# Two plain f pairs instead of one at the start of each FFN, the first token half first

## The chip, the cores and the metric

The kernel runs on one core of a Trainium2 chip. The metric is the device time of one execution in microseconds (us). The engines are called as the profile calls them: PE (matrix multiply; PEld is its weight load), DVE (vector), ACT (scalar), POOL (GpSimd), SP (the queue that issues all DMAs here).

## The reference, cut to what matters

One transformer block on 1024 tokens of 1024 features in float32: an FFN, a token mixer (two attentions, untouched by this change), a second FFN, a last norm. The change is in the first stage of both FFNs.

```python
def rmsnorm(x, g):
    y = xf * lax.rsqrt(jnp.mean(xf * xf, axis=-1, keepdims=True) + EPS)
    return y * g
def swiglu(h, w1, w3, w2):                 # w1, w3: 1024 x 2816, w2: 2816 x 1024
    return (jax.nn.silu(h @ w1) * (h @ w3)) @ w2
...
    x = x + 0.5 * swiglu(rmsnorm(x, ffn1_norm[l]), ffn1_w1[l], ffn1_w3[l], ffn1_w2[l])
    x = x + token_mix(rmsnorm(x, mix_norm[l]), ...)
    x = x + 0.5 * swiglu(rmsnorm(x, ffn2_norm[l]), ffn2_w1[l], ffn2_w3[l], ffn2_w2[l])
```

## The kernel before

Activations lie with features on the 128 partitions: eight feature tiles k of 128 x 512 for each of two token halves tb (K.x[tb][k]). A float32 product is done as three matmuls: each operand is split into a rounded part hi (ACT copies it, L86) and the rest lo (DVE subtracts, L82), and mm3 (L48) adds hi·hi, hi·lo and lo·hi into one PSUM bank. So "a product over all k" is 24 matmuls of 128 x 512.

**ffn_up (L250) computes silu(h w1) · (h w3)** for 22 tiles f of 128 hidden columns, in 11 pairs of f.

- *The first pair is plain* (L266 to L286): for tb = 0, then tb = 1, for both f, banks u[0] (w1) and u[1] (w3) get 24 matmuls each: 96 matmuls in a half, 192 in the pair. Its weights come as four tiles ws[n] of 512 KB (load_fresh, L193): a DMA into one of two staging buffers (wst), a split into whi and wlo. The first half (tb = 0) does not wait for the norm: it multiplies x·gain, and its results are scaled by R[0] = 1/rms afterwards (L278, L280). The first FFN has these weights loaded ahead (`first`), between the loads of x.
- *The second half needs the normed input.* scale_h (L199) makes x·gain·R for the second half on DVE (L209) and splits it (ACT L86, DVE lo L82); then the same for the first half, with ACT (L206) and POOL (L207) doing the scaling.
- *The other ten pairs are done with seven products instead of eight* (L301 to L343, Strassen-Winograd on 2 x 2 blocks: token halves by feature halves). That needs the sums of input blocks made by right_sums (L226: DVE L239 and L243, POOL L241 and L245, 16 splits into tiles `tf`), in place in the x tiles, and sums of weight blocks (L327 to L330; s1, a21, a11, s4), on DVE in the first such pair, on POOL later. A product is 24 matmuls (L298), so such a pair takes 168 matmuls. Banks X, Y, Z hold two banks each.
- *What sets the order.* The program is written in the order above, but the framework's scheduler puts the instructions of each engine into a fixed order by its own timeline estimate, and adds the waits. Each engine and each DMA queue then runs its list strictly in order. Buffers are reused: a tile waits until the last reader of what lay there has finished. The plain part's results go through banks X (f = 0) and Y (f = 1), in both halves. The raw weight tiles of the seven-product pairs (L291, L292: a21, a22, s1, s4) lie where the x tiles were, so their loads wait for the last reads of x.

ffn_down (L356) multiplies by w2 and is not touched; the mixer neither.

The lines that put the first pair into order:

```python
        for tb in range(NTB):
            for f in range(2):
                u = [bank("XY"[f], m) for m in range(2)]
                ...
            if tb == 0:
                scale_h(K, 0, gi, scale_h(K, 1, gi))
        T = right_sums(K, tp)
```

Of the kernel before, what the change touches and what calls it, by code (L numbers as in the profile page):

```python
# [7 lines left out]
F32 = mybir.dt.float32  # L8
F32R = mybir.dt.float32r
# [6 lines left out]
P = 128  # L16
T = 1024
TB = 512
NTB = 2
HB = 256  # L20
D = 1024
KD = 8
NF = 22
# [17 lines left out]
def open_pool(K, ctx, name, bufs, psum=False, side=None):  # L41
    kw = {"space": PSUM} if psum else {}
    if side:
        kw["side"] = side
    return ctx.enter_context(K.tc.tile_pool(name=name, bufs=bufs, reuse_waits="tile", **kw))
# [39 lines left out]
def split(nc, hi, lo, src):  # L85
    nc.scalar.activation(out=hi, in_=src, func=AF.Copy)  # L86
    return lo_of(nc, lo, src, hi)
# [105 lines left out]
def load_fresh(K, n, src):  # L193
    st = K.wst.tile([P, KD, P], F32, tag="wst", name="wst")
    K.nc.sync.dma_start(out=st, in_=src)
    return split_fresh(K, n, st)
# [29 lines left out]
def right_sums(K, tp):  # L226
    nc = K.nc
    h = KD // 2
    T = [[], [], [], []]

# [6 lines left out]
    for k in range(h):  # L237
# [8 lines left out]
        put(3, k, b21)  # L246
    return T


def ffn_up(K, w13, tp, ctx0, gi, first):  # L250
    nc = K.nc
    h = KD // 2
    ctx = ExitStack()
    ps = open_pool(K, ctx, "up_ps", 1, True, side="right")
    bank = lambda n, m: ps.tile([P, TB], F32, tag=f"{n}{m}", name=n)
    K.nw = 0

    def form(src):
        hi, lo = split_fresh(K, K.nw, src)
        K.nw += 1  # L260
        return hi, lo

    def store(f, tb, t):
        nc.sync.dma_start(out=K.s_a[tb][f], in_=t)

    with ExitStack() as c1:  # L266
        sb = open_pool(K, c1, "up_s", 3, side="right")
        ws = first if first else [load_fresh(K, n, w13[n // 2, n % 2]) for n in range(4)]
        K.nw = 4
        for tb in range(NTB):  # L270
            for f in range(2):
                u = [bank("XY"[f], m) for m in range(2)]
                for m in range(2):
                    for k in range(KD):
                        mm3(nc, u[m], ws[2 * f + k // h], m * h + k % h, K.h[tb][k], k == 0, k == KD - 1)
                t = sb.tile([P, TB], F32, tag="s", name="s")
                if tb == 0:
                    nc.vector.tensor_tensor(out=t, in0=u[0], in1=K.R[0], op=ALU.mult)  # L278
                    order_after(K, nc.scalar.activation(out=t, in_=t, func=AF.Silu), K.rdone)
                    nc.gpsimd.tensor_tensor(out=t, in0=t, in1=K.R[0], op=ALU.mult)  # L280
                else:
                    nc.scalar.activation(out=t, in_=u[0], func=AF.Silu)
                nc.vector.tensor_tensor(out=t, in0=u[1], in1=t, op=ALU.mult)
                store(f, tb, t)
            if tb == 0:
                scale_h(K, 0, gi, scale_h(K, 1, gi))  # L286
        T = right_sums(K, tp)
    ctx0.close()
    with ctx:
        rw = open_pool(K, ctx, "up_raw", 1)  # L290
        po = open_pool(K, ctx, "up_post", 1)  # L291
        raw = lambda n: rw.tile([P, KD, P], F32, tag=n, name=n)  # L292
        B11, B21, B22 = K.h[0][0:h], K.h[0][h:], K.h[1][h:]

        def prod(o, w, m, x, start):
            for k in range(h):
                for i, (a, b) in enumerate(((0, 0), (0, 1), (1, 0))):
                    nc.tensor.matmul(o, lhsT=w[a][:, m * h + k], rhs=x[k][b], start=start and k == 0 and i == 0,  # L298
                                     stop=k == h - 1 and i == 2, skip_group_check=True)

        for fp in range(1, NF // 2):  # L301
            f0, f1 = 2 * fp, 2 * fp + 1
            a11 = K.wst.tile([P, KD, P], F32, tag="wst", name="a11")
            a12 = K.wst.tile([P, KD, P], F32, tag="wst", name="a12")
            a21, a22, s1, s4 = raw("a21"), raw("a22"), raw("s1"), raw("s4")
            for t, f, j in ((a11, f0, 0), (a21, f1, 0), (a22, f1, 1), (a12, f0, 1)):
                nc.sync.dma_start(out=t, in_=w13[f, j])
            u = {}
            for n in ("s1", "u2", "u3", "c21", "c11"):
                for m in range(2):  # L310
                    if n != "c11" or m == 0:
                        u[n, m] = po.tile([P, TB], F32, tag=f"{n}{m}", name=n)
            X, Y, Z = [[bank(n, m) for m in range(2)] for n in "XYZ"]

            w = form(a11)
            for m in range(2):
                prod(X[m], w, m, B11, True)
                nc.scalar.activation(out=u["s1", m], in_=X[m], func=AF.Copy)
            w = form(a12)
            for m in range(2):  # L320
                prod(X[m], w, m, B21, False)
            c = u["c11", 0]
            nc.scalar.activation(out=c, in_=X[0], func=AF.Silu)
            nc.vector.tensor_tensor(out=c, in0=X[1], in1=c, op=ALU.mult)
            store(f0, 0, c)
            se = nc.vector if fp == 1 else nc.gpsimd
            se.tensor_tensor(out=s1, in0=a21, in1=a22, op=ALU.add)  # L327
            se.tensor_tensor(out=a21, in0=a11, in1=a21, op=ALU.subtract)
            se.tensor_tensor(out=a11, in0=s1, in1=a11, op=ALU.subtract)
            se.tensor_tensor(out=s4, in0=a12, in1=a11, op=ALU.subtract)  # L330
            for src, x, n in ((a11, T[1], "u2"), (a21, T[2], "u3"), (a22, T[3], "c21")):
                w = form(src)
                for m in range(2):
                    prod(Y[m], w, m, x, n == "u2")
                    nc.vector.tensor_tensor(out=u[n, m], in0=Y[m], in1=u["s1", m], op=ALU.add)
                if n == "c21":
                    finish_a(K, u[n, 0], u[n, 1], f1, 0, store)
            for src, x, n, f in ((s1, T[0], "u3", f1), (s4, B22, "u2", f0)):
                w = form(src)
                for m in range(2):  # L340
                    prod(Z[m], w, m, x, n == "u3")
                    nc.vector.tensor_tensor(out=u[n, m], in0=Z[m], in1=u[n, m], op=ALU.add)  # L342
                finish_a(K, u[n, 0], u[n, 1], f, 1, store)  # L343
# [77 lines left out]
def ffn(K, w13, w2, ctx0, gi, first, xsrc, after, tail=None):  # L421
    with ExitStack() as ctx:
        if not first:
            K.wpools = [K.whl, open_pool(K, ctx, "whl2", B_W, side="right")]
        with ExitStack() as c1:
            ffn_up(K, w13, open_pool(K, c1, "tf", 1, side="right"), ctx0, gi, first)
        ffn_down(K, w2, xsrc, after, tail)


# [1002 lines left out]
```

## Time and profile before

| | us |
|---|---|
| median of 3 runs | 3072.87 (3072.54 to 3073.18) |
| the profiled execution's own time | 3074.79 |
| its span, first to last instruction | 3072.7 |
| mean granted PE clock over the span | 0.982 |
| PE busy | 2925.8 (95%) |
| DVE / ACT / POOL busy | 1838.1 / 1267.6 / 842.3 |

The profiled execution took 1.92 us more than the median, and 2.09 us of it lie around its span. In a timeline row the first number is the start, the second how long the merged piece lasts; "[7.27 <-ACT hi L86]" says that the engine stood idle for 7.27 us before it and what ended that. Matmul pieces show 0.39 us for one, but they are pipelined: what counts is the distance from start to start.

### The profile page before, as it was taken

The page shows a single profiled execution, that of the slowest core. Times are in us where ns is not written, and L with a number is a line of the kernel's source. Part 1 is how long each engine was busy: PE and PEld are TensorE (multiplying, and loading weights), DVE is VectorE, ACT ScalarE, POOL GpSimd, SP SyncE. Part 2 cuts the span into 40 slices and gives each one's busy share as a digit, 9 for nine tenths or more (in the row PEclk, how much of TensorE's full clock was granted, in tenths as well). Part 3 has the DMA queues.
Part 4 walks back from the last instruction along what each step waited for, and adds up shares of the span by engine and source line. Part 5 has one row for each costly group of instructions (what it writes and reads, how often), then busy time and mean ns, then how long its engine had stood idle before and what let it go on. Part 6 is the DMA issues. An engine that isn't in the chain of part 4 may idle for free.

```text
span 3072.7 us, 39792 instructions
## 1 busy us (share of the span) xinstructions
PE 2925.8 (95%) x14490; PEld 2442.3 (79%) x14490; DVE 1838.1 (60%) x3057; ACT 1267.6 (41%) x2231; POOL 842.3 (27%) x687
## 2 busy tenths in 40 slices
PE   6999999999999999889899999999999899999998
PEld 5788887887888778777788888888777688887887
DVE  7655554445678467667677777766434855555354
ACT  6222223332323245345566666666434322223342
POOL 5333330000035222322233333222332433331000
PEclk9999999999999999999999999999999999999999
DMA  2222226444546645444432234222832122225442
GB/s 103 93 83 83 82 69 235 159 144 140 158 158 224 214 142 181 162 168 155 140 111 83 83 123 149 83 76 89 303 124 91 56 83 83 82 83 199 154 167 66
DMA packets 168643, 397.95 MB, mean 130 GB/s; under 512 B 16000, under 2 KB 34688, under 8 KB 168448
## 3 DMA queue, kind: packets, MB, share of 16 engines
q1 hardware_dynamic: 168448, 395.42, 38.0%
q8 instruction: 114, 1.87, 0.3%
q14 instruction: 81, 0.66, 0.1%
HBM read 274.77 MB, written 120.59 MB: 129 GB/s over the span
## 4 chain that ended last, share of the span: by engine, by line
PE 78%; DVE 8%; DMA 6%; ACT 3%; issue 3%; POOL 2%; SPq 1%; DVEq 0%; ACTq 0%; POOLq 0%
PE Y L298 11%; PE X L298 7%; PE Z L298 7%; PE gm L49 6%; PE gm L51 6%; PE gm L50 6%; PE S L682 6%; PE acc L49 5%; PE acc L51 5%; PE acc L50 5%; PE tr L732 3%; PE o L886 2%; PE o L885 2%; DMA sg<-smx 1%; DMA wst<-in_win_dram 1%
## 5 line engine op out<-in xcount | busy, mean ns | idle before, releaser
L82 DVE TENSOR_TENSOR wlo<-wst,whi 128x1024 fp32r<-128x1024 f32 x183 | 238.1, 1303 | 233.6 <-ACT whi L86 223.3
L49 PE MATMUL gm<-hi,whi 128*128 128x512 f32 x880 | 352.5, 401 | 4.6 <-ACT whi L86 2.1
L51 PE MATMUL gm<-hi,wlo 128*128 128x512 f32 x880 | 348.9, 397 | 0.0
L50 PE MATMUL gm<-lo,whi 128*128 128x512 f32 x880 | 348.6, 396 | 0.0
L682 PE MATMUL S<-kt,qt 128*128 128x320 f32 (+5 forms) x1152 | 274.5, 352 | 44.2 <-ACT Pt L691 16.5
L298 PE MATMUL Y<-tf,whi 128*128 128x512 f32 x960 | 300.2, 394 | 1.0 <-ACT whi L86 1.0
L86 ACT ACTIVATE whi<-wst 128x1024 fp32r<-128x1024 f32 x147 | 155.1, 1058 | 333.0 <-PE acc L50 187.3
L86 ACT ACTIVATE th<-tr 128x512 fp32r<-128x512 f32 (+2 forms) x384 | 204.0, 543 | 200.9 <-PE tr L732 196.5
L82 DVE TENSOR_TENSOR tl<-tr,th 128x512 fp32r<-128x512 f32 (+2 forms) x384 | 236.6, 620 | 82.6 <-ACT th L86 78.9
L49 PE MATMUL acc<-ah,whi 128*128 128x512 f32 (+1 forms) x728 | 280.4, 385 | 4.5 <-DVE u L342 4.5
L51 PE MATMUL acc<-ah,wlo 128*128 128x512 f32 (+1 forms) x728 | 280.3, 385 | 0.0
L50 PE MATMUL acc<-al,whi 128*128 128x512 f32 (+1 forms) x728 | 279.7, 384 | 0.0
L689 DVE CUSTOM_DVE_ANT_0 S<-S,slab 128x896 f32<-128x896 f32 (+7 forms) x320 | 224.9, 709 | 69.3 <-PE S L682 64.0
L682 PEld LDWEIGHTS S<-kt,qt 128*128 128x128 f32 x1152 | 183.5, 190 | 67.8 <-ACT Pt L691 17.7
L839 POOL TENSOR_SCALAR Ps<-Ps,l 128x384 f32<-128x384 f32 (+7 forms) x128 | 100.7, 787 | 422.3 <-DVE l L837 209.9
L298 PEld LDWEIGHTS Y<-tf,whi 128*128 128x128 f32 x960 | 180.7, 188 | 43.0 <-ACT whi L86 1.4
L86 ACT ACTIVATE whi<-a 128x1024 fp32r<-128x1024 f32 x100 | 104.0, 1058 | 233.4 <-PE Y L298 157.7
L49 PEld LDWEIGHTS gm<-hi,whi 128*128 128x128 f32 x880 | 168.6, 192 | 37.5 <-ACT whi L86 2.3
L51 PEld LDWEIGHTS gm<-hi,wlo 128*128 128x128 f32 x880 | 168.2, 191 | 36.0 <-DVE wlo L82 0.3
L50 PEld LDWEIGHTS gm<-lo,whi 128*128 128x128 f32 x880 | 168.3, 191 | 31.5 <-issue 0.5
L82 DVE TENSOR_TENSOR wlo<-a,whi 128x1024 fp32r<-128x1024 f32 x100 | 173.9, 1753 | 26.3 <-ACT whi L86 26.3
L298 PE MATMUL Y<-tf,wlo 128*128 128x512 f32 x480 | 188.6, 394 | 0.0
(302 smaller groups left out, 6683.4 us busy)
## 6 DMA issues: line engine op xcount, KB each, us to landing
wst<-in_win_dram SPq DMA_DIRECT2D x55, 512.0 KB
wst<-in_f1w_dram SPq DMA_DIRECT2D x48, 512.0 KB
wst<-in_f2w_dram SPq DMA_DIRECT2D x48, 512.0 KB
ar<-sa SPq DMA_DIRECT2D x88, 256.0 KB
a<-in_f1w_dram SPq DMA_DIRECT2D x40, 512.0 KB
a<-in_f2w_dram SPq DMA_DIRECT2D x40, 512.0 KB
qt<-sq SPq DMA_DIRECT2D x128, 128.0 KB
qt<-sqn SPq DMA_DIRECT2D x64, 256.0 KB
```

The lines of the kernel that those rows point to most:

```text
L49: first = nc.tensor.matmul(out, lhsT=w[0][:, wk], rhs=x[0], start=start, stop=False, skip_group_check=skip)
L50: nc.tensor.matmul(out, lhsT=w[0][:, wk], rhs=x[1], start=False, stop=False, skip_group_check=skip)
L51: nc.tensor.matmul(out, lhsT=w[1][:, wk], rhs=x[0], start=False, stop=stop, skip_group_check=skip)
L82: return nc.vector.tensor_tensor(out=lo, in0=src, in1=hi.bitcast(F32), op=ALU.subtract)
L86: nc.scalar.activation(out=hi, in_=src, func=AF.Copy)
L298: nc.tensor.matmul(o, lhsT=w[a][:, m * h + k], rhs=x[k][b], start=start and k == 0 and i == 0, stop=k == h - 1 and i == 2, skip_group_chec ...
L682: K.last = nc.tensor.matmul(S[:, o:o + n], lhsT=q, rhs=k[:, k0 + c:k0 + c + n], start=i == 0, stop=i == 1)
L689: nc.vector.tensor_tensor_reduce(out=sv, in0=sv, in1=mv, scale=-0.125, scalar=BIG, op0=ALU.add, op1=ALU.min, accum_out=nm)
L732: nc.tensor.transpose(tr[:, b * P:(b + 1) * P], src, K.ident)
L839: nc.gpsimd.tensor_scalar(out=p[:, 0:n], in0=p[:, 0:n], scalar1=l[:, c:c + 1], scalar2=1.0, op0=ALU.mult, op1=ALU.mult)
L885: nc.tensor.matmul(dst, lhsT=v, rhs=hi[:, b * P:(b + n) * P], start=False, stop=False, skip_group_check=True)
L886: nc.tensor.matmul(dst, lhsT=v, rhs=lo[:, b * P:(b + n) * P], start=False, stop=last, skip_group_check=True)
```

## The change

Two pairs are done plainly instead of one (NPLAIN = 2), eight weight tiles instead of four, and both pairs are done on the first token half before the second half is touched: the order of (tb, pair) is (0,0), (0,1), (1,1), (1,0). The weights of the second pair get a pool of their own (up_w, four pairs of tiles), which is closed before the pool `tf` of the block sums is opened: the sums lie where these weights were. The results go round the three bank sets X, Y, Z. The second half is scaled after (0,0), the first half (in place of its own unscaled split) after (0,1). Nine pairs are left for the seven-product form.

```diff
+def load_plain(K, pools, n, src):
+    st = K.wst.tile([P, KD, P], F32, tag="wst", name="wst")
+    K.nc.sync.dma_start(out=st, in_=src)
+    pool = pools[n % 2] if n < 4 else pools[2]
+    hi = pool.tile([P, KD, P], F32R, tag="whi", name="whi")
+    lo = pool.tile([P, KD, P], F32R, tag="wlo", name="wlo")
+    split(K.nc, hi, lo, st)
+    return hi, lo
+
+NPLAIN = 2
...
-        sb = open_pool(K, c1, "up_s", 3, side="right")
-        ws = first if first else [load_fresh(K, n, w13[n // 2, n % 2]) for n in range(4)]
-        K.nw = 4
-        for tb in range(NTB):
+        plain = K.wpools[:]
+        plain.append(open_pool(K, c1, "up_w", 4, side="right"))
+        sb = open_pool(K, c1, "up_s", 3)
+        ws = [first if first else [load_plain(K, plain, n, w13[n // 2, n % 2]) for n in range(4)]]
+        ws.append([load_plain(K, plain, n, w13[n // 2, n % 2]) for n in range(4, 8)])
+        nu = 0
+        for tb, p in ((0, 0), (0, 1), (1, 1), (1, 0)):
             for f in range(2):
-                u = [bank("XY"[f], m) for m in range(2)]
+                nu += 1
+                u = [bank("XYZ"[nu % 3], m) for m in range(2)]
                 for m in range(2):
                     for k in range(KD):
-                        mm3(nc, u[m], ws[2 * f + k // h], m * h + k % h, K.h[tb][k], k == 0, k == KD - 1)
+                        mm3(nc, u[m], ws[p][2 * f + k // h], m * h + k % h, K.h[tb][k], k == 0, k == KD - 1)
...
-                store(f, tb, t)
-            if tb == 0:
-                scale_h(K, 0, gi, scale_h(K, 1, gi))
-        T = right_sums(K, tp)
+                store(2 * p + f, tb, t)
+            if (tb, p) == (0, 0):
+                gates = scale_h(K, 1, gi)
+            if (tb, p) == (0, 1):
+                scale_h(K, 0, gi, gates)
+    K.nw = 4
+    T = right_sums(K, open_pool(K, ctxt, "tf", 1, side="right"))
...
-        for fp in range(1, NF // 2):
+        for fp in range(NPLAIN, NF // 2):
...
-            se = nc.vector if fp == 1 else nc.gpsimd
+            se = nc.vector if fp == NPLAIN else nc.gpsimd
```

In the changed file the lines stand lower: L278 is L295, L283 is L300, L298 is L318, L307 is L327, L327 is L347; L49 to L245 are the same.

**The order of PE, first FFN, where the first token half ends.** hi_276, lo_277 and hi_349, lo_350 are the first and the last feature tile of the first half's input, whi_271 to wlo_337 the first pair's weights, whi_420 and wlo_421 the first tile of the second pair's. Before:

```order
L50 MATMUL Y_475<-lo_350,whi_336 128x512
L51 MATMUL Y_475<-hi_349,wlo_337 128x512
L49 MATMUL X_618<-hi_531,whi_271 128x512 [waits Activation_49]
L49 MATMUL X_619<-hi_531,whi_271 128x512 [waits DVE_49]
L49 MATMUL Y_672<-hi_531,whi_314 128x512
L49 MATMUL Y_673<-hi_531,whi_314 128x512 [waits DVE_49]
L50 MATMUL X_618<-lo_532,whi_271 128x512 [waits DVE_49]
```

The same place now, and then the end of the second pair's first half:

```order
L50 MATMUL Z_499<-lo_350,whi_336 128x512
L51 MATMUL Z_499<-hi_349,wlo_337 128x512
L49 MATMUL X_594<-hi_276,whi_420 128x512 [waits Activation_49]
L50 MATMUL X_594<-lo_277,whi_420 128x512
L51 MATMUL X_594<-hi_276,wlo_421 128x512
...
L51 MATMUL Y_651<-hi_349,wlo_439 128x512
L49 MATMUL Z_754<-hi_555,whi_420 128x512 [waits Activation_49]
L50 MATMUL Z_754<-lo_556,whi_420 128x512 [waits DVE_49]
```

Before, the second half's input (hi_531, lo_532) was asked for right behind the first half. Now 96 matmuls on the first half's input stand between, and the second half's first tile (hi_555, lo_556) is asked for behind them.

**The order of DVE, first FFN, up to the scaling of the second half.** R_360 and R_402 are 1/rms of the halves; nm, nacc their steps. Before:

```order
L162 TENSOR_SCALAR nm_358<-tot_356 128x512 [waits PE_49]
L120 TENSOR_TENSOR nacc_280<-nacc_280,nm_358 128x512 [waits DVE_49,Activation_49]
L121 TENSOR_SCALAR nacc_280<-nacc_280 128x512 [waits DVE_49]
L122 TENSOR_TENSOR R_360<-R_360,nacc_280 128x512 [waits DVE_49]
L162 TENSOR_SCALAR nm_400<-tot_398 128x512 [waits PE_49]
L278 TENSOR_TENSOR s_468<-X_418,R_360 128x512 [waits DVE_49]
```

And now:

```order
L82 TENSOR_TENSOR wlo_421<-wst_418,whi_420 128x1024 [waits DMAHW5_49,Activation_49]
L151 TENSOR_TENSOR nacc_368<-nacc_368,nsq_395 128x512 [waits DVE_49,Activation_49]
L162 TENSOR_SCALAR nm_358<-tot_356 128x512 [waits PE_49]
L82 TENSOR_TENSOR wlo_427<-wst_424,whi_426 128x1024 [waits DMAHW6_49,Activation_49]
L120 TENSOR_TENSOR nacc_280<-nacc_280,nm_358 128x512 [waits DVE_49,Activation_49]
L121 TENSOR_SCALAR nacc_280<-nacc_280 128x512 [waits DVE_49]
L82 TENSOR_TENSOR wlo_433<-wst_430,whi_432 128x1024 [waits DMAHW7_49,Activation_49]
L122 TENSOR_TENSOR R_360<-R_360,nacc_280 128x512 [waits DVE_49]
L162 TENSOR_SCALAR nm_400<-tot_398 128x512 [waits PE_49]
L82 TENSOR_TENSOR wlo_439<-wst_436,whi_438 128x1024 [waits DMAHW0_49,Activation_49]
L295 TENSOR_TENSOR s_492<-Y_442,R_360 128x512 [waits DVE_49]
```

The four splits of the second pair's weights now stand inside the chain that makes R, each waiting for its load.

**The order of DVE, first FFN, the block sums.** tf tiles are the splits of the block sums, s_858 is the result of (1,1) with f = 1, s_912 that of (1,0) with f = 0, a11 the first seven-product weight. Now:

```order
L243 TENSOR_TENSOR x1_7_267<-x1_7_267,x0_3_264 128x512 [waits Pool_49]
L300 TENSOR_TENSOR s_804<-Z_755,s_804 128x512 [waits DMAHW4_49,PE_49,Activation_49]
L300 TENSOR_TENSOR s_858<-X_809,s_858 128x512 [waits DMAHW5_49,PE_49,Activation_49]
L82 TENSOR_TENSOR tf_977<-x0_0_252,tf_976 128x512 [waits Activation_49]
...
L82 TENSOR_TENSOR tf_1047<-x1_7_267,tf_1046 128x512 [waits Activation_49]
L82 TENSOR_TENSOR wlo_1090<-a11_1064,whi_1089 128x1024 [waits DMAHW1_49,PE_49,Activation_49]
L300 TENSOR_TENSOR s_912<-Y_863,s_912 128x512 [waits DMAHW6_49,PE_49]
```

Before, these splits stood mixed with the sums themselves, from the first sum on. Now twelve of them follow in one row behind the last result of (1,1).

In the mixer, between the two FFNs, no engine's order changes.

## Rows read from the trace of the kernel before

**Rows 1.** The page: busy time by engine, and the shares of the chain that ended last.

```profile
PE 2925.8 (95%) x14490; PEld 2442.3 (79%) x14490; DVE 1838.1 (60%) x3057; ACT 1267.6 (41%) x2231; POOL 842.3 (27%) x687
...
PE 78%; DVE 8%; DMA 6%; ACT 3%; issue 3%; POOL 2%; SPq 1%; DVEq 0%; ACTq 0%; POOLq 0%
```

**Rows 2.** The timeline of PE, first FFN: the rows at which it stops and goes on (start, length, what, idle before it).

```profile
32.45 0.39 PE L51 MATMUL Y<-hi,wlo 128*128 128x512 f32 x1
40.10 1.22 PE L49 MATMUL X<-hi,whi 128*128 128x512 f32 x2 [7.27 <-ACT hi L86]
...
47.72 0.79 PE L49 MATMUL Y<-hi,whi 128*128 128x512 f32 x1 [5.97 <-DVE s L283]
48.80 0.79 PE L50 MATMUL X<-lo,whi 128*128 128x512 f32 x1 [0.29 <-DVE lo L82]
...
72.05 0.50 PE L298 MATMUL X<-hi,whi 128*128 128x512 f32 x1 [0.25 <-ACT whi L86]
...
80.15 0.79 PE L298 MATMUL X<-hi,wlo 128*128 128x512 f32 x1 [7.37 <-DVE wlo L82]
...
81.17 0.63 PE L298 MATMUL X<-lo,whi 128*128 128x512 f32 x1
81.60 0.63 PE L298 MATMUL X<-hi,wlo 128*128 128x512 f32 x1
...
94.58 1.20 PE L298 MATMUL Z<-tf,whi 128*128 128x512 f32 x4 [0.91 <-ACT whi L86]
96.74 1.20 PE L298 MATMUL Y<-tf,whi 128*128 128x512 f32 x4 [0.96 <-ACT whi L86]
99.06 0.54 PE L298 MATMUL Z<-tf,wlo 128*128 128x512 f32 x1 [1.12 <-DVE wlo L82]
...
475.35 0.40 PE L298 MATMUL Z<-hi,wlo 128*128 128x512 f32 x1
```

**Rows 3.** The chain that ended last, first FFN, in order of time (start, length, what): from the second half's norm to the first seven-product matmuls.

```profile
38.26 8.81 DVE x L209 x8
...
47.66 10.87 DVE lo L82 x10
...
59.21 7.70 POOL x L241
...
78.96 1.15 DVE wlo L82
```

**Rows 4.** The instructions of L298 alone in the steady stretch of the first FFN (window, its length, PE busy (count), PEld busy (count), granted clock, DMA share, GB/s).

```profile
126.67:476.00 349.33, 349.07 (x1513) 283.43 (x1511) 1.00 0.25 82
```

**Rows 5.** All engines in a stretch of the first FFN in which PE waits (columns: us, PE, PEld, DVE, ACT, POOL busy with counts, granted clock, DMA share, GB/s).

```profile
40.00:50.00 10.00, 3.64 (x7) 2.12 (x8) 10.00 (x10) 9.67 (x19) 8.38 (x6) 0.50 0.07 26
```

**Rows 6.** The timeline of PE, second FFN.

```profile
2357.76 0.47 PE L49 MATMUL X<-hi,whi 128*128 128x512 f32 x1
...
2380.81 0.61 PE L49 MATMUL X<-hi,whi 128*128 128x512 f32 x2
2385.54 0.50 PE L50 MATMUL X<-lo,whi 128*128 128x512 f32 x1 [4.12 <-DVE lo L82]
...
2409.33 0.39 PE L298 MATMUL X<-hi,whi 128*128 128x512 f32 x1
...
2411.83 0.39 PE L298 MATMUL X<-hi,wlo 128*128 128x512 f32 x1
2416.19 0.50 PE L298 MATMUL X<-hi,whi 128*128 128x512 f32 x1 [3.98 <-DVE s L283]
...
2424.51 0.50 PE L298 MATMUL X<-hi,whi 128*128 128x512 f32 x1 [0.66 <-ACT s L318]
...
2432.08 2.08 PE L298 MATMUL Z<-tf,whi 128*128 128x512 f32 x4 [4.50 <-ACT whi L86]
...
2811.11 0.40 PE L298 MATMUL Z<-hi,wlo 128*128 128x512 f32 x1
```

**Rows 7.** Loads of 512 KB: the SP queue's issues in the first FFN (two of a, the first when the first buffer is free), and one piece of the chain in the second FFN (issue to landing of two such loads together).

```profile
18.50 6.42 SPq L307 DMA_DIRECT2D a<-in_f1w_dram  x2
...
2422.98 4.41 DMA a<-in_f2w_dram
```

**Rows 8.** The timeline of DVE: splits of weights (wlo), of the second half's input (lo) and of block sums (tf), and its idle time in the norm's chain of the first FFN.

```profile
23.35 1.22 DVE L82 TENSOR_TENSOR wlo<-wst,whi 128x1024 fp32r<-128x1024 f32 x1
25.75 1.49 DVE L151 TENSOR_TENSOR nacc<-nacc,nsq 128x512 f32<-128x512 f32 x2 [1.18 <-POOL nacc L151]
...
29.86 0.69 DVE L120 TENSOR_TENSOR nacc<-nacc,nm 128x512 f32<-128x512 f32 x1 [2.03 <-ACT nacc L119]
...
47.59 10.94 DVE L82 TENSOR_TENSOR lo<-x,hi 128x512 fp32r<-128x512 f32 x10
...
59.05 0.68 DVE L82 TENSOR_TENSOR lo<-x,hi 128x512 fp32r<-128x512 f32 x1
59.65 0.68 DVE L239 TENSOR_TENSOR x<-x,x 128x512 f32<-128x512 f32 x1
...
68.63 3.49 DVE L82 TENSOR_TENSOR tf<-x,tf 128x512 fp32r<-128x512 f32 x2
```

**Rows 9.** The timeline of POOL, first FFN: scalings of the first half beside the splits of rows 8.

```profile
48.42 6.55 POOL L207 TENSOR_TENSOR x<-x,R 128x512 f32<-128x512 f32 x4 [0.22 <-ACT x L206]
```

**Rows 10.** Groups of DVE instructions from 36 to 90 us (count | busy us, mean ns | idle before).

```profile
L82 DVE TENSOR_TENSOR tf<-x,tf 128x512 fp32r<-128x512 f32 x16 | 14.6, 954 | 0.0
```

More of the change, by code (lines that the diff above doesn't have):

```diff
@@ L247, in right_sums, with ffn_up @@
     return T
-def ffn_up(K, w13, tp, ctx0, gi, first):
+def load_plain(K, pools, n, src):
[7 more added lines that the diff above has]
+NPLAIN = 2
+def ffn_up(K, w13, ctxt, ctx0, gi, first):
     nc = K.nc
@@ L425, in ffn @@
         with ExitStack() as c1:
-            ffn_up(K, w13, open_pool(K, c1, "tf", 1, side="right"), ctx0, gi, first)
+            ffn_up(K, w13, c1, ctx0, gi, first)
         ffn_down(K, w2, xsrc, after, tail)
```

## The prediction

> **What bounds the kernel.** PE is busy for 95% of the span and holds 78% of the chain that ended last [rows 1]. So a change pays where PE stands idle or runs slowly, and costs where PE gets more matmuls. I went from the page to PE's timeline at the beginning of each FFN, for its holes and what ended them; to the chain of waits there, for what fills the holes; to the timelines of DVE, POOL and SP, for what the new order asks of them; and to the order of the changed program, for what is late next.
>
> In the first FFN PE ends the plain pair's first half at 32.7 us and then stands still for 7.27 us, does four matmuls, stands still for 5.97 us, and again for 7.37 us behind the second matmul of the seven-product part [rows 2]. The chain shows why: norm, 8.81 us of scaling on DVE, 10.87 us of splits, then sums, then the split of a weight that is queued behind them [rows 3]. From 40 to 50 us DVE is busy all the time and PE for 3.64 us [rows 5]. After a hole PE also runs at half its clock for some microseconds: the granted clock is 0.50, the 1.2 GHz level, in the stretch with the holes [rows 5], and after the last one matmuls start 0.43 us apart [rows 2]. The second FFN has the same holes, shorter: 4.12, 3.98, 0.66 and 4.50 us [rows 6]. Elsewhere the seven-product part is dense: 1513 matmuls from 126.67 to 475.58 us, **0.2306 us each** [rows 2, 4]. I use that pitch throughout.
>
> **What the change adds.** A plain pair has 192 matmuls, a seven-product pair 168. So each FFN gets 24 more: 24 x 0.2306 = 5.5 us, all on PE, 11.1 us in both. Further splits and results of the plain pair on DVE, ACT and POOL take the place of weight sums and results of the pair they replace; they count only where they delay the chain (below). DMA traffic is the same eight weight tiles, moved earlier.
>
> **What it removes.** 96 matmuls that need nothing new are put where PE had to wait. I compare the moment at which the seven-product part ends.
>
> First FFN, before: 32.7 us to the end of the first half, end at 475.6 us [rows 2]. In between lie 96 + 1680 matmuls, 409.5 us at the steady pitch; so 33.4 us are lost, of which the holes listed in rows 2 make 24.1 and slow matmuls behind them the rest. After, without any hole: 32.7 + 288 x 0.2306 = 99.1 us to the end of the plain pairs, + 1512 x 0.2306 = 348.7, end at 447.8 us. **Gain 27.8 us**, the 24 added matmuls included.
>
> Second FFN, before: first half ends at 2380.8, the end is at 2811.3 us [rows 6]; less 409.5 us that leaves 21.0 us lost. After: 2380.8 + 66.4 + 348.7 = 2795.9. **Gain 15.4 us.** Together 43.2 us, if PE never waits.
>
> **Does it never wait?** I put the new order's lists beside the durations, place by place.
>
> *The second pair's weights.* Four more tiles of 512 KB go through the two staging buffers, ahead of the loads of a. The first can be issued at 18.5 us, when a buffer is free; two loads took 4.41 us together [rows 7], so I take 2.2 to 4.4 us for one. The first is split by about 26 to 28 us, the last by 36 to 38; PE asks for them at 32.7, 35.5, 43.8 and 46.5. No wait.
>
> *The norm's chain in the first FFN.* These four splits (1.13 us each on DVE, about what [rows 8] shows start to start) now stand inside it, and ACT and DVE wait in order for the loads. Part falls into DVE's idle time of 1.18 and 2.03 us [rows 8]. Walking down both lists, the scaling begins at 40.3 us (short loads) to 42.5 us (long ones) in place of 38.3 [rows 3]. Add 8.8 us of scaling and two results: the eight splits lo of the second half begin at 50.3 to 52.5 us. With ten of them in 10.94 us [rows 8] the last is ready at 59 to 61.2. PE comes to the second half at 32.7 + 22.1 = 54.8 and needs the last of the eight tiles at 59.7. So between 0 and 1.5 us of waiting; I take 1.5, since these loads meet those of x.
>
> *The same in the second FFN.* R is made later there, since DVE waits for a product of POOL ahead of it: scaling begins at 2380.4 to 2381.6, the last split is done by 2402.3; PE comes at 2403.0 and needs that one at 2407.7. No wait.
>
> *The first half's new splits* may be written only when (0,1) has been read, and have the 22.1 us of (1,1) for some 14 DVE instructions of 0.6 to 1.1 us: no wait.
>
> *The block sums' splits* lie where the second pair's weights were, so they begin after (1,1), at 77 us in the first FFN, with the 22.1 us of (1,0) before them. Twelve splits at 0.95 us [rows 10], two results and two weight splits take some 15 us; PE needs the first weight at 99.1 and the first sum 11 us later. Then the loads of a21 and a22 wait for the last four splits: issued by 97, landed 4.41 us later [rows 7], three sums and a split: ready at about 106, needed at 110. No wait. The bank set of (1,1), X, is free long before the seven-product part begins on it: that wait of 3.98 us [rows 6] ends.
>
> For small waits in the first seven-product pairs I add 0.5 us. **Sum:** 43.2 - 1.5 - 0.5 = 41.2 us. The profiled execution took 3074.79 us, so the sum gives 3033.6 on its terms; the median of the runs is 1.92 us lower, and I predict **3031.7 us** against 3072.87. Ends of this case: no wait at all (3029.7) and the 576 plain matmuls still to come at 0.227 us, the pitch of twelve matmuls from 2409.33 to 2411.83 [rows 6], 3027; waits three times as long, 3036.
>
> **Rivals.**
>
> *POOL holds up the splits.* The eight splits of the second half run beside POOL's eight scalings of 1.64 us [rows 9]. Alone a split takes 0.60 us from start to start, beside POOL ten take 10.94 us, 1.09 each [rows 8]: the 4.9 us more are three whole POOL instructions among ten splits. If the new order lines them up so that each split waits for a whole POOL instruction, eight take 8 x (0.60 + 1.64) = 17.9 us in place of 8.7, 9.2 us later. The first FFN has no reserve left: 9 us of holes more, and about 1 us of half clock; in the second, with 5 us in reserve, 4 us go. 3031.7 + 14.2 = **3046**. Against it: before, the same instructions stood side by side and most passed. It decides from the third held split on; each further one costs up to 1.64 us. Chance 0.10. The Trainium skill ("SBUF — State Buffer", Who interferes with whom) says that a DVE instruction with two inputs there and a GpSimd instruction that reads it lock each other out for the whole instruction; by that rule this case comes about if the starts interleave one by one, and the 1.09 us agree with it only as a mean of held and free ones.
>
> *The sums are late again.* The twelve splits in a row may meet POOL's last sums and run at 1.75 us, as two did [rows 8], and the raw weights come behind them; then the holes before the second kind of product return: 7.37, 0.91, 0.96 and 1.12 us in the first FFN [rows 2], 0.66 and 4.50 in the second [rows 6], 15.5 us: **3047**. For it: DVE is full in this stretch [rows 5] and the splits are bound to a shorter window. Against it: 6 us of reserve in the first FFN, as worked out. Chance 0.06.
>
> *The loads come too late: slower.* The new weights' loads stand ahead of R on ACT and DVE, both of which run in order. If the second half's first split comes as late behind PE's new place as it did before (32.7 to 48.8 us, 16 us [rows 2]), every hole is back and only the 24 matmuls per FFN are left: 3072.87 + 11.1 = **3084**. That takes a split at 70.9 us in place of 51.4 to 53.6, so loads some 17 us longer in a chain of two loads, over 8 us each more than the 4.41 us seen for two. Nothing in rows 7 is near it. Chance 0.02.
>
> *The order is not what the text says.* The scheduler could have left the second half in front. The printed order shows 96 matmuls on the first half in between; this rival is out.
>
> **How the numbers follow.** Forecast 0.80, POOL 0.10, late sums 0.06, slower 0.02; 0.02 for a mixture that eats most of the gain. The range goes from 3027 up to 3047, where it takes in the first two rivals and leaves out little. Differences under 0.2% (6.1 us) can hardly be told from none here: faster 0.96, same 0.02, slower 0.02.
>
> **What would show it.** After: PE without a hole over 1 us from 6.5 us to the end of both plain pairs, save one or a few waits for DVE lo around 55 to 61 us; first seven-product matmul at about 99 to 102 us and end of that part at 448 to 451 us; in the second FFN 66 us from the end of the first half to the first seven-product matmul, no wait of X for a result, and 15 us less in all; clock at its full level from 10 us on. 14490 + 48 matmuls. Wrong would be: a hole of more than 5 us at the beginning of (1,1) (then the chain to R or POOL), or at the third bank set's first sums (then the sums), or a longer pitch in the nine pairs.

## The result, and the profile after

The change ran in **3033.66 us** (median of 4 runs, 3032.19 to 3036.29), the kernel before in the same session in 3073.02: a ratio of 0.9869, 95% interval 0.9852 to 0.9886. That is 40 us (35 to 45) less; predicted were 41.2. Run again later beside experiments, it took 3026.68 us, a ratio of 0.9854 (0.9837 to 0.9870). The profiled execution took 3032.19 us, its span is 42.3 us shorter than that of the profiled execution before.

The page of the change, its span, busy times and the shares of the chain that ended last:

```profile
span 3030.4 us, 39832 instructions
PE 2923.3 (96%) x14538; PEld 2443.4 (81%) x14538; DVE 1816.8 (60%) x3041; ACT 1258.6 (42%) x2221; POOL 814.0 (27%) x677
PE 81%; DMA 6%; DVE 5%; ACT 3%; issue 3%; POOL 2%; SPq 1%; DVEq 0%; ACTq 0%; POOLq 0%
```

Against [rows 1], PE has 48 matmuls more and a span that is 42 us shorter; its share of the chain went from 78% to 81%. The chain still goes through PE; what left it is waiting (DVE's share went from 8% to 5%).

All waits of PE from 0 to 460 us in the change (engine, tile, line, what it waited for: us in all, times, longest):

```profile
PE Y L49 <- ACT hi L132: 6.5, 1, 6.5
PE Z L50 <- DVE lo L82: 1.0, 2, 0.7
PE acc L49 <- DVE u L362: 0.9, 1, 0.9
```

The first is the start of the program, as before. Of the holes of 7.27, 5.97 and 7.37 us in [rows 2] none is left. PE's timeline in the first FFN of the change (start, length, what, idle before it):

```profile
6.50 1.22 PE L49 MATMUL Y<-hi,whi 128*128 128x512 f32 x2 [6.50 <-ACT hi L132]
...
12.24 0.99 PE L49 MATMUL Y<-hi,whi 128*128 128x512 f32 x2
13.07 0.39 PE L50 MATMUL Y<-lo,whi 128*128 128x512 f32 x1
...
33.75 0.39 PE L49 MATMUL X<-hi,whi 128*128 128x512 f32 x1
...
44.95 0.39 PE L49 MATMUL Y<-hi,whi 128*128 128x512 f32 x1
...
56.15 0.39 PE L49 MATMUL Z<-hi,whi 128*128 128x512 f32 x1
...
59.63 0.50 PE L50 MATMUL Z<-lo,whi 128*128 128x512 f32 x1 [0.29 <-DVE lo L82]
...
61.33 0.50 PE L50 MATMUL Z<-lo,whi 128*128 128x512 f32 x1 [0.72 <-DVE lo L82]
...
450.68 0.39 PE L318 MATMUL Z<-hi,wlo 128*128 128x512 f32 x1
450.90 0.40 PE L49 MATMUL acc<-ah,whi 128*128 128x512 f32 x1
...
454.27 0.50 PE L49 MATMUL acc<-ah,whi 128*128 128x512 f32 x1 [0.87 <-DVE u L362]
```

Up to 13.07 us the matmuls start mostly 0.43 us apart, from there about 0.23. From 33.75 to 56.15 us PE does the 96 matmuls of (0,1), where before it stood still for most of the time. At 56.15 it begins the second half and has to wait twice for splits lo, 1.0 us in all. The nine pairs end at 450.90 us, against 475.58 before (the last start in [rows 2] and one pitch).

The second FFN, same view: the first matmul, the ends of (0,0) and (0,1), the first seven-product matmul, the end of the nine pairs:

```profile
2331.69 0.47 PE L49 MATMUL Y<-hi,whi 128*128 128x512 f32 x1
...
2354.73 0.39 PE L49 MATMUL X<-hi,whi 128*128 128x512 f32 x1
...
2377.13 0.39 PE L49 MATMUL Z<-hi,whi 128*128 128x512 f32 x1
...
2421.60 0.39 PE L318 MATMUL X<-hi,whi 128*128 128x512 f32 x1
...
2770.34 0.40 PE L49 MATMUL acc<-ah,whi 128*128 128x512 f32 x1
```

From the end of the first half to the end of the nine pairs: 415.61 us, against 2380.81 to 2811.34 = 430.53 before [rows 6]. It starts 26.07 us earlier than before.

DVE's scaling of the second half and its splits lo in the change, first FFN:

```profile
42.04 8.94 DVE L209 SCALAR_TENSOR_TENSOR x<-x,gain,R 128x512 f32<-128x512 f32 x8
...
52.10 10.37 DVE L82 TENSOR_TENSOR lo<-x,hi 128x512 fp32r<-128x512 f32 x8
```

Eight splits in 10.37 us, 1.30 each in the mean, where ten took 10.94 before [rows 8]. The mean hides two kinds; two of the eight by themselves:

```profile
52.10 0.68 DVE L82 TENSOR_TENSOR lo<-x,hi 128x512 fp32r<-128x512 f32 x1
...
54.40 1.78 DVE L82 TENSOR_TENSOR lo<-x,hi 128x512 fp32r<-128x512 f32 x1
```

Five of the eight take 1.77 or 1.78 us and last 1.70 from start to start, each with a POOL instruction beside it; the first and the last two take 0.68, 0.60 from start to start. It was much the same before: of the first eight of the ten, four came 1.70 apart and one 1.08, and the eight took 9.7 us.

### The profile page after: what moved, and what is told of

Read it like the earlier page. It is cut to its first block, busy times and chain, and to the rows that moved or that the text cites. A ratio compares the mean times of both kernels' runs of the same rounds, so it can differ in the third digit from the quotient of the medians.

```text
span 3030.4 us, 39832 instructions
## 1 busy us (share of the span) xinstructions
PE 2923.3 (96%) x14538; PEld 2443.4 (81%) x14538; DVE 1816.8 (60%) x3041; ACT 1258.6 (42%) x2221; POOL 814.0 (27%) x677
## 4 chain that ended last, share of the span: by engine, by line
PE 81%; DMA 6%; DVE 5%; ACT 3%; issue 3%; POOL 2%; SPq 1%; DVEq 0%; ACTq 0%; POOLq 0%
PE Y L318 10%; PE X L318 7%; PE gm L49 6%; PE Z L318 6%; PE gm L51 6%; PE gm L50 6%; PE S L702 6%; PE acc L49 5%; PE acc L51 5%; PE acc L50 5%; PE tr L752 3%; PE o L906 2%; PE o L905 2%; DMA sg<-smx 1%; PE po L50 1%
## 5 line engine op out<-in xcount | busy, mean ns | idle before, releaser
L82 DVE TENSOR_TENSOR wlo<-wst,whi 128x1024 fp32r<-128x1024 f32 x191 | 247.9, 1300 | 242.7 <-ACT whi L86 234.2
L49 PE MATMUL gm<-hi,whi 128*128 128x512 f32 x880 | 352.5, 401 | 4.3 <-ACT whi L86 1.9
L86 ACT ACTIVATE whi<-wst 128x1024 fp32r<-128x1024 f32 x155 | 163.7, 1058 | 342.7 <-PE acc L50 189.9
L49 PE MATMUL acc<-ah,whi 128*128 128x512 f32 (+1 forms) x728 | 280.4, 385 | 1.7 <-DVE u L362 1.7
L318 PE MATMUL Y<-tf,whi 128*128 128x512 f32 x864 | 269.3, 393 | 0.0
L49 PEld LDWEIGHTS gm<-hi,whi 128*128 128x128 f32 x880 | 168.2, 191 | 37.2 <-ACT whi L86 2.1
L318 PEld LDWEIGHTS Y<-tf,whi 128*128 128x128 f32 x864 | 162.2, 188 | 37.2
L86 ACT ACTIVATE whi<-a 128x1024 fp32r<-128x1024 f32 x90 | 93.5, 1059 | 219.4 <-PE Y L318 156.7
L318 PE MATMUL Y<-tf,wlo 128*128 128x512 f32 x432 | 169.7, 394 | 0.0
L82 DVE TENSOR_TENSOR wlo<-a,whi 128x1024 fp32r<-128x1024 f32 x90 | 153.2, 1716 | 24.7 <-ACT whi L86 24.4
```

Source lines behind the costliest of these rows:

```text
L49: first = nc.tensor.matmul(out, lhsT=w[0][:, wk], rhs=x[0], start=start, stop=False, skip_group_check=skip)
L82: return nc.vector.tensor_tensor(out=lo, in0=src, in1=hi.bitcast(F32), op=ALU.subtract)
```

## The experiments

The theory: the gain is holes of PE filled with 96 matmuls per FFN that need nothing new, less 24 added ones, and the norm's chain on DVE is hidden behind them, barely in the first FFN and well in the second. Rivals: the third bank set or the larger amount of plain work pays, whatever the order; or the gain is made in one FFN alone.

Medians of one kernel differed by some microseconds between sessions (the change: 3033.66 and 3026.68). So the parts are read from the traces. In us, from the first matmul of an FFN to the end of its pairs, and what lies between:

| kernel | first FFN | between | second FFN |
|---|---|---|---|
| before | 469.06 | 1882.18 | 453.58 |
| the change | 444.40 | 1880.79 | 438.65 |
| change_again | 443.95 | 1878.59 | 438.68 |
| second_only | 469.65 | 1877.75 | 438.69 |
| in_turn | 461.46 | 1876.70 | 451.43 |
| two_sets | 448.99 | 1884.79 | 445.68 |
| later | 449.67 | 1884.29 | 438.66 |
| pool_free | 441.87 | 1877.32 | 438.69 |
| z_first | 443.11 | 1871.09 | 438.66 |
| both | 443.42 | 1878.59 | 438.68 |

The second FFN repeats to 0.04 us wherever its PE does not wait. The stage between, where these kernels have the same work save the wait of the accumulators (none to 2.3 us at its beginning), moves by 13.7 us; that is what makes differences of a few microseconds unreadable in the medians. It is the mixer that moves: from its first matmul to the second FFN it takes 1621.6 us in z_first and 1633.7 in later. The down projection ahead of it, from its first accumulation to that matmul, repeats to 0.04 us wherever the bank sets are first used in the same order: 251.9 us in before and second_only, 250.6 in the change, change_again, in_turn, later and pool_free, 249.4 to 249.5 in z_first and both (253.4 in two_sets).

### The second FFN alone

ffn_up_old is the first stage of the kernel before; its text is left out here.

```diff
+def ffn_up_old(K, w13, tp, ctx0, gi, first):
...
-            ffn_up(K, w13, c1, ctx0, gi, first)
+            if first:
+                ffn_up_old(K, w13, open_pool(K, c1, "tf", 1, side="right"), ctx0, gi, first)
+            else:
+                ffn_up(K, w13, c1, ctx0, gi, first)
```

> Only the second FFN has the new beginning; the first FFN is as before. My theory (each FFN gains by its own filled holes, with nothing carried over): the second FFN's part is worth 14.9 us and the earlier accumulators behind it 1.4 us, so 16.3 us less than before, about 3056.7 us (3054 to 3059); first FFN in the trace ends its seven-product part at 475.6 us as before, the second one's takes 438.7 us from the end of the first half. Rival (the gain is made in one place, the first FFN, and the second only follows it): about 3073 us, or 3033 us the other way round.

Measured: 3054.53 us (5 runs), ratio to before 0.9942 (0.9929 to 0.9954), so 18 us less (14 to 22). The first FFN keeps its old length and its old holes, the second has the change's to 0.04 us. PE's waits in this kernel's first FFN, the three longest after the start and that of the accumulators:

```profile
PE X L49 <- ACT hi L86: 7.5, 1, 7.5
PE X L311 <- DVE wlo L82: 7.4, 1, 7.4
...
PE Y L49 <- DVE s L296: 6.0, 1, 6.0
PE acc L49 <- DVE u L355: 2.3, 1, 2.3
```

Each FFN gains for itself; the gain in one place is out.

### The pairs one after the other

```diff
-        for tb, p in ((0, 0), (0, 1), (1, 1), (1, 0)):
+        for tb, p in ((0, 0), (1, 0), (0, 1), (1, 1)):
```

> Both plain pairs, the third bank set and the own weight tiles are kept, but the pairs are asked for one after the other: (0,0), (1,0), (0,1), (1,1). The scheduler itself still puts 20 and 21 matmuls of (0,1) into the hole. My theory (what pays is the 96 matmuls of the first half standing in front of the second half): the holes before the second half come back, in the first FFN 10 us to the first split hi and 4 to 8 us for the splits lo, in the second 1.5 and 3.5 to 7 us; the block sums' splits now wait for the last plain matmul, since they lie where the second pair's weights are, and give a further hole of 5 to 10 us per FFN. With some microseconds of half clock that is 30 to 44 us more than the change: 3064 to 3078 us, most or all of the gain lost. Rival (the gain comes from the third bank set and from having more plain work between the splits and the seven-product part, whatever the order): 3034 to 3045 us.

Measured: 3059.09 us, ratio 0.9954 (0.9941 to 0.9966), 12 us less than before. Some 70% of the gain is gone, not nearly all. By the table 7.6 and 2.2 us of the 24.7 and 14.9 us in the two FFNs stay, a quarter. PE's timeline, first FFN of this kernel:

```profile
37.74 0.77 PE L49 MATMUL Z<-hi,whi 128*128 128x512 f32 x1 [4.27 <-DVE s L295]
...
45.58 0.62 PE L49 MATMUL X<-hi,whi 128*128 128x512 f32 x2
46.03 0.61 PE L49 MATMUL Y<-hi,whi 128*128 128x512 f32 x2
50.68 0.80 PE L49 MATMUL Z<-hi,whi 128*128 128x512 f32 x1 [4.03 <-DVE s L300]
```

I had expected PE to stand for 10 us before the second half. The scheduler had pulled not 20 but 44 matmuls of (0,1) forward (from 37.74 and from 50.68 us), so it filled part of the hole even in this order, and each of its two pieces had to wait for a bank that R held. The sums' holes came back as 0.2, 0.9, 1.0 and 1.1 us, less than my 5 to 10; with what follows them the nine pairs take 5.9 us longer than in the change in the first FFN and 3.1 in the second. Neither my range nor the rival's held the time: the order makes most of the gain, and what is left without it, a quarter to 30%, contains work that the scheduler put into the hole by itself.

### Two bank sets

```diff
-                u = [bank("XYZ"[nu % 3], m) for m in range(2)]
+                u = [bank("XY"[nu % 2], m) for m in range(2)]
```

> The change with two bank sets (X, Y in turn) for the plain pairs in place of three. My theory: in the first FFN (0,1) must wait for the first result's read, which needs R: from 33.8 to about 37.9 us, 4.1 us; the wait for the last splits lo (1.0 us) goes in return. In the second FFN (0,1)'s second f waits some 4 us for a read that stands behind the scaling on DVE. Both seven-product parts begin on X right behind a plain result on X, 2 to 4 us each. Sum 10 to 16 us: 3044 to 3050 us. Rival (the third set is not needed, since PE has 22 us of other work between two uses of a set): 3033 to 3036 us.

Measured: 3046.40 us, ratio 0.9918 (0.9904 to 0.9932). In the table 4.6 to 5.0 us more in the first FFN and 7.0 in the second. PE's waits, one of the first FFN and then those of the second:

```profile
PE Y L49 <- DVE s L295: 4.7, 1, 4.7
...
PE X L49 <- DVE s L300: 4.0, 1, 4.0
PE acc L49 <- DVE u L362: 2.3, 1, 2.3
```

In the first FFN that is the wait for `s L295`, the first read that needs R, until 38.32 us (4.1 until 37.9 expected), and the wait for lo goes in return. The waits of the seven-product part for X, 2 to 4 us in my sum, did not come; in their place the accumulators wait 2.3 us in both FFNs, and the 4.0 us cost 7.0 with the slow matmuls behind them. So the time lies in my range, but by another sum than mine. The third set is part of the gain.

### The scaling later

```diff
+    for _ in range(0 if gates else 8):
+        nc.vector.tensor_scalar(out=K.R[tb], in0=K.R[tb], scalar1=1.0, scalar2=0.0, op0=ALU.mult, op1=ALU.add)
```

> The change, with eight small DVE instructions on R of the second half (multiplied by one, in place) ahead of its scaling, 0.60 us each from start to start: the scaling begins up to 4.8 us later in both FFNs. My theory: the first FFN has no reserve left (PE waits 1.0 us for the last splits lo), so it pays all of it, 3.5 to 5.5 us in waits for lo at the beginning of (1,1); the second FFN has its last lo ready at 2374.4 where PE needs it at 2382, so it pays nothing. 3037 to 3039.5 us. Rival A (the chain is hidden in both): 3033 to 3035 us. Rival B (it is the bound in both): 3043 us.

Measured: 3039.28 us, ratio 0.9888 (0.9873 to 0.9904). First FFN 5.3 to 5.7 us longer, second the same to 0.02. PE in the first FFN of this kernel:

```profile
56.03 0.39 PE L49 MATMUL Z<-hi,whi 128*128 128x512 f32 x1
58.68 0.50 PE L50 MATMUL Z<-lo,whi 128*128 128x512 f32 x1 [2.26 <-DVE lo L82]
60.38 0.79 PE L50 MATMUL Z<-lo,whi 128*128 128x512 f32 x1 [0.74 <-DVE lo L82]
```

and the engines in two stretches around and behind these waits (us, busy of PE, PEld, DVE, ACT, POOL with counts, granted clock, DMA share, GB/s):

```profile
58.00:66.00 8.00, 6.46 (x13) 3.47 (x14) 8.00 (x7) 4.67 (x9) 6.61 (x5) 0.61 0.08 33
66.00:74.00 8.00, 8.00 (x35) 6.41 (x34) 8.00 (x10) 2.79 (x5) 3.60 (x3) 0.96 0.01 2
```

The first of these stretches in the change itself:

```profile
58.00:66.00 8.00, 6.99 (x29) 5.05 (x28) 7.97 (x9) 2.89 (x6) 4.33 (x3) 1.00 0.09 35
```

The waits grew only by 2.0 us, from 1.0 to 3.0, where I had expected 3.5 to 5.5 more: in the 8 us around them the granted clock is 0.61, a mean of the 1.2 and the 2.4 GHz level, so PE gets slow, and a slow PE meets the later splits nearly without waiting. The 96 matmuls of (1,1) take 29.4 us (56.03 to 85.41), 7.0 more than those of (0,1), where the change took 1.5 more; its clock stayed at 1.00. The price is about the one forecast, but a list of waits shows less than half of it. The eight instructions cost DVE more than the 4.8 us of my estimate: the last lo comes 5.3 us later than in the change (67.79, not 62.48), and 5.8 later in the second FFN, counted from its first matmul. There it comes at 2389.1 us and PE needs it at about 2390.9: of a reserve of some 7.6 us 5.8 are used. The last three splits of this kernel there:

```profile
2386.16 2.98 DVE L82 TENSOR_TENSOR lo<-xx,hi 128x512 fp32r<-128x512 f32 x3
```

The chain is the bound in the first FFN alone.

### POOL kept away from the splits

```diff
+        s = nc.vector.scalar_tensor_tensor(out=x, in0=x, scalar=g, in1=K.R[tb], op0=ALU.mult, op1=ALU.mult)
         if gates:
-            order_after(K, nc.scalar.activation(out=x, in_=x, func=AF.Copy, scale=g), gates[k])
-            nc.gpsimd.tensor_tensor(out=x, in0=x, in1=K.R[tb], op=ALU.mult)
-        else:
-            nc.vector.scalar_tensor_tensor(out=x, in0=x, scalar=g, in1=K.R[tb], op0=ALU.mult, op1=ALU.mult)
+            order_after(K, s, gates[-1])
```

The change itself ran beside it and the next two:

> The change itself, unaltered, beside the next three in the same session: 3033.7 us again (3031 to 3037).

> The change, with the first half's eight scalings done by DVE behind the second half's splits lo in place of POOL beside them. My theory (the splits lo run at 1.30 us in place of 0.60 because POOL's scalings stand beside them): the eight lo take 5 to 5.5 us in place of 10.37 and 10.92, the scaling of the second half too gets shorter (8.94 us by up to 3); the last lo is ready at 54 to 58 us, before PE comes at 56.15; both waits of PE for lo (1.0 us) and the half microsecond of slow matmuls behind them go. First FFN 1.5 us shorter, second FFN unchanged: 3032 us, the difference to be read from the first FFN's place in the trace and not from the medians. Rival (the splits are slow for another reason, such as waiting for ACT's hi): lo stay at 1.2 us or more and the waits stay or grow. Second rival (DVE is too full now): the first half's splits come after 78 us and a new wait stands at the beginning of (1,0); 3036 us or more.

Measured: change_again 3026.68 us, ratio 0.9854 (0.9837 to 0.9870); pool_free 3027.77 us, ratio 0.9858 (0.9843 to 0.9872), the same. From the end of the first half to the end of the nine pairs the first FFN takes 415.62 us (33.05 to 448.67), where the change took 417.15 and 416.82: 1.2 to 1.5 us less, and PE has no wait for lo. DVE of this kernel, first FFN:

```profile
41.21 5.80 DVE L205 SCALAR_TENSOR_TENSOR x<-x,gain,R 128x512 f32<-128x512 f32 x8
...
48.13 4.89 DVE L82 TENSOR_TENSOR lo<-x,hi 128x512 fp32r<-128x512 f32 x8
52.94 6.42 DVE L205 SCALAR_TENSOR_TENSOR x<-x,gain,R 128x512 f32<-128x512 f32 x8
...
60.48 4.89 DVE L82 TENSOR_TENSOR lo<-x,hi 128x512 fp32r<-128x512 f32 x8
65.30 1.28 DVE L237 TENSOR_TENSOR x<-x,x 128x512 f32<-128x512 f32 x2
```

and POOL:

```profile
39.04 2.78 POOL L295 TENSOR_TENSOR s<-s,R 128x512 f32<-128x512 f32 x2 [13.19 <-ACT s L294]
48.95 5.22 POOL L295 TENSOR_TENSOR s<-s,R 128x512 f32<-128x512 f32 x1 [7.13 <-ACT s L294]
61.30 6.43 POOL L295 TENSOR_TENSOR s<-s,R 128x512 f32<-128x512 f32 x1 [7.13 <-ACT s L294]
```

With POOL's scalings away, scaling takes 5.80 us in place of 8.94 and the splits 4.89 in place of 10.37, 0.60 each. The edit takes ACT's scalings away too, but no split of the change had idle time of DVE before it, so none was waiting for ACT: POOL was what made five of them slow. It holds the other way too: the POOL instruction that begins at 48.95 us beside the train of splits ends 1.15 us after it (54.17, and 48.13 + 4.89 = 53.02); it takes 5.22 us where two others take 2.78. The next one begins beside the train from 60.48 us and ends 1.15 us after that (67.73, and 65.30 + 1.28 = 66.58). The Trainium skill ("SBUF — State Buffer", Who interferes with whom) calls this an exclusive lock on a shared port pair, which the one that issues first gets for its whole instruction while the other blocks. The trace agrees that each holds up the other, but not with the order, since six splits that start after 48.95 us end before the POOL instruction that starts there does (by a profile in which POOL's spans are rough).

### Z first, and both edits

```diff
-                u = [bank("XYZ"[nu % 3], m) for m in range(2)]
+                u = [bank("ZYX"[(nu - 1) % 3], m) for m in range(2)]
```

> The change, with the plain pairs' results in the bank sets Z, Y, X in turn in place of Y, Z, X, so that the set Z, which the seven-product part reads last, gets the banks that were asked for first. My theory of the unpredicted 1.4 us per FFN (the accumulators of the down projection take the banks in the order in which the sets were first used; with Y, Z, X three accumulators can begin before the first bank of Z is met, with X, Y, Z only one): with Z first five can begin, and the wait of the accumulators for the last sum, 0.87 us in each FFN, goes: 1.7 us less, 3032 us, read from the waits. Rival (the wait depends only on when the last sum is done): 0.87 us stays. Second rival (Z first is the wrong way round): 2.3 us or more, as in before.

> The two edits together: DVE scales the first half, and the bank sets go Z, Y, X. If both theories hold, the gains add: 1.5 + 1.7 = 3.2 us less than the change, 3030.5 us, no wait of PE over 0.3 us in either FFN's first part from the first matmul to the tenth accumulation of the down projection. If the first falls and the second holds: 3032 us.

Measured: z_first 3027.29 us, ratio 0.9855 (0.9836 to 0.9874); both 3026.76 us, ratio 0.9852 (0.9838 to 0.9867). PE's waits in the first FFN of z_first:

```profile
PE Z L49 <- ACT hi L132: 6.8, 1, 6.8
PE Y L50 <- DVE lo L82: 0.5, 1, 0.5
```

The accumulators' wait of 0.87 us is gone, in both FFNs (the second has no wait at all). So it hangs on the order in which the sets are first used: X, Y, Z (before) and Y, X with Z last (two_sets) give 2.27, Y, Z, X 0.87, Z, Y, X none. Between fixed points that is worth 1.3 us per FFN from the first to the second of these orders and 1.2 from the second to the third, by the down projections given above. In `both` the first FFN's pairs take 415.61 us from the end of the first half, like the second's. The last four kernels cannot be told apart by their medians; the trace shows `both` 2.9 to 3.3 us shorter than the change in its parts (1.2 to 1.5 in the first FFN, and two waits of 0.87), 0.1%, and I claim no more for it.

The medians themselves were missed: change_again took 3026.68 where 3031 to 3037 was expected, and pool_free, z_first and both lie 3.7 to 4.7 us under their 3032, 3032 and 3030.5, though the kernel before took 3071.99 beside them, only 1.0 less than in the first session. Of the 2.5 us between the two profiled executions of the change 2.2 lie in the mixer; what made it shorter stays open.

## Why the prediction was right, point by point

**First FFN, 27.8 us less 1.5 for waits.** Measured 24.7 from first matmul to last (475.58 to 450.90 at equal starts). Two terms make the 1.6 us that are missing from 26.3. The first half ended 1.07 us later, because the slow pitch of the start lasted to 13.07 us in the change (10 was foreseen) and to 10.56 before:

```profile
10.13 0.63 PE L49 MATMUL X<-hi,whi 128*128 128x512 f32 x1
10.56 0.43 PE L50 MATMUL X<-lo,whi 128*128 128x512 f32 x1
10.83 0.39 PE L51 MATMUL X<-hi,wlo 128*128 128x512 f32 x1
```

That is not the change's: its 96 first matmuls took 27.25 us, and five other executions with the same ones 26.25 (pool_free) to 27.81 us (both). And the second pair runs at 11.20 us for 48 matmuls (33.75 to 44.95), 0.2333 us each and not 0.2306, which makes 0.5 us; why this pair is slower stays open.

The waits came at the place foreseen, 1.0 us in the list and 0.5 more, and 1.5 was foreseen. The 0.5 is not a low clock, which was granted at 1.00 there: the list counts a gap from the modelled end of the matmul before it, 0.39 us after its start where the pitch is 0.23, and the matmul behind each of the two gaps is followed after 0.35 us. That the number came out so exactly is luck: PE reached the second half 1.35 us later than foreseen (56.15, not 54.8), and the last lo was ready 1.3 us later than the long end of its range. The 0.5 us for small waits in the first seven-product pairs was not needed.

**The chain of the norm.** Foreseen: scaling begins at 40.3 to 42.5 us, lo at 50.3 to 52.5, last lo ready at 59 to 61.2. Seen: 42.04, 52.10, 62.5. The last is late because I took 1.09 us for one split, the mean of ten in which more were free of POOL, and read the rest as three whole POOL instructions among ten. The rows one by one show something else: four or five of the first eight were held before, and five in the change, each lasting 1.70 us from start to start together with the POOL instruction beside it, and not 0.60 + 1.64 = 2.24. So the rival's mechanism was at work in both kernels, and its price was too high: the eight took 10.37 us, 4.89 without POOL, and all eight held would be 8 x 1.70 = 13.6 by this estimate, not 17.9. POOL's share of the change's chain is 5.5 us of splits and 3.1 of scaling, of which PE felt 1.2 to 1.5 in the first FFN.

**Second FFN, 15.4 us.** Measured 14.9; the 0.5 is the same pitch of 0.2333. Scaling began 22.85 us after the first matmul (2354.54 less 2331.69), foreseen 22.6 to 23.8; no wait, and a reserve that `later` measured.

**Weights, first half's splits, block sums, raw weights:** no wait of PE between 61.33 us and the accumulators, as foreseen; the first seven-product matmul came at 102.16 (99 to 102), the end at 450.90 (448 to 451). 348.74 us for nine pairs, foreseen 348.7.

**What was not foreseen:** the accumulators' wait went from 2.27 us before to 0.87 in each FFN, by the order of the bank sets. The row of before:

```profile
478.82 0.50 PE L49 MATMUL acc<-ah,whi 128*128 128x512 f32 x1 [2.27 <-DVE u L342]
```

Between fixed points that is 1.3 us in each FFN. So 24.7 + 14.9 + 2.6 = 42.2 us of the 42.3 by which the spans differ, against 41.2: a gain that I had missed covers what the start and the pitch cost, and that is luck. So is it that the mixer took the same in these two executions to 0.1 us, where it moves by 12 between kernels; by the medians the gain was 39.4 us in one session and 45.3 in the other. The 24 added matmuls cost 6.0 us per FFN (a plain pair 44.8, a seven-product pair 348.74 / 9 = 38.75), not 5.5. The low end of the forecast, 3027, is 0.8 us under what its own terms give, without consequence.

**The other rivals.** Late sums: no such wait in the change; in_turn, which binds their splits to a later moment, shows them at 3.2 us of waits in the first FFN and 2.2 in the second. Loads too late: all eight weights were there when PE asked, and `later` shows that a last lo 5.3 us later cost 5.3 to 5.7, far from the whole gain.

## What to carry to other kernels

When PE waits for a chain on slower engines, look for work on data that is ready and price it by the hole: here 96 matmuls in front of the second half of each FFN won 39.6 us though 48 were added, and a bank set that is not held by the late factor is part of the deal. A list of waits understates a hole: waits of 1.0 us cost 1.5 at full clock, one of 4.0 cost 7.0, and waits of 3.0 in all cost 7.0 where the clock fell; compare the times of fixed points instead. Where DVE carries the critical chain with two-input instructions, keep POOL off that stretch: here the splits ran in half the time once DVE did POOL's share behind them, though only 1.2 to 1.5 us of that reached PE. And read a mean of merged instructions one by one before it is used as a price: 1.09 us was a mixture of splits at 0.60 and at 1.70.

## What the runs showed of the hardware

A single POOL instruction beside a closed train of two-input DVE instructions took 5.22 us in one place and 6.43 in another where two others took 2.78 together (POOL's spans are rough in this profile, but both end 1.15 us behind the train). A row of POOL instructions, on the other hand, alternated with the DVE splits, 1.70 us from start to start in place of 0.60, for five of eight. Why a lone one gets through late and a row of them in turn stays open. Around waits of 2.26 and 0.74 us the granted clock was 0.61 over 8 us; around waits of 0.29 and 0.72 us it stayed at 1.00. A wait of 4.0 us cost 7.0 in all; the 8 us behind it ran at a granted clock of 0.59. The slow pitch at the beginning of the program ended at 10.56 us before and at 13.07 in the change with the same matmuls; what decides that stays open, as does the 12 us by which the mixer moved: its granted clock was 0.98 in the longest and 0.99 in the shortest, which goes the right way, but no run tests it.
